# Output weights and affine residual rows: where in the kernel they are prepared

## The chip, the cores and the metric

One core of a Trainium2 chip runs the whole program in one launch. Its engines are TensorE (PE: matmuls; PEld: its weight loads), VectorE (DVE), ScalarE (ACT), GpSimd (POOL) and SyncE (SP); in this kernel SP and POOL mostly issue DMA transfers. The metric is the device time of one execution in microseconds (us). The kernel before took 2729.65 us, the median of three runs (2724.99 to 2732.59).

## What is computed

A decoder trunk of two layers over 1024 rows of width 1024, in float32. Each layer is a token mixer followed by a dense MLP, each in a residual LayerNorm:

```python
for i in range(DEPTH):
    shift, scale, gate = ada_mod(c, ada_w[i, 0], ada_b[i, 0])
    h = x * (1.0 + scale) + shift
    y = mixer_a(h, ...) if i % N_MIXERS == 0 else mixer_b(h, b_w_qkv[j], b_w_out[j], slopes)
    x = layer_norm(ALPHA * x + gate * y, ln_g[i, 0], ln_b[i, 0])
    shift, scale, gate = ada_mod(c, ada_w[i, 1], ada_b[i, 1])
    h = x * (1.0 + scale) + shift
    y = squared_relu_mlp(h, mlp_w_up[i], mlp_w_down[i])
    x = layer_norm(ALPHA * x + gate * y, ln_g[i, 1], ln_b[i, 1])
```

The change lies in the second layer's mixer, an attention with three window patterns:

```python
def mixer_b(h, w_qkv, w_out, slopes):
    qkv = (h @ w_qkv).reshape(B, S, N_PAT, 3, B_HEADS, B_HEAD_DIM)
    for g, (window, dilation) in enumerate(B_PATTERNS):
        o, lse = dilated_branch(qkv[:, :, g, 0], qkv[:, :, g, 1], qkv[:, :, g, 2], window, dilation, slopes)
    wts = jax.nn.softmax(jnp.stack(lses, axis=0), axis=0)[..., None]
    o = jnp.sum(wts * jnp.stack(outs, axis=0), axis=0)
    return o.reshape(B, S, B_HEADS * B_HEAD_DIM).astype(h.dtype) @ w_out
```

Two things of it matter here. `w_out` (called `b_w_out` in the kernel) is multiplied by the gate before the product, since `gate * (o @ w_out)` is `o @ (w_out * gate)`. And the residual `ALPHA * x` is rebuilt from rows that were stored normalised but without LayerNorm's gain and bias: `row * (ALPHA * ln_g[0, 1]) + ALPHA * ln_b[0, 1]`. These last are the affine rows.

## The kernel before

**Numbers in two parts.** Each float32 operand of a matmul is split into a high part (a ScalarE cast, line 102) and a low part (a VectorE subtraction, line 103); a product is three matmuls, high by high, high by low and low by high. `split` is that helper, so many groups in the profile have lines 102 and 103, and the tile's name tells them apart.

**The stages.** First the mixer of layer one, then its MLP (`psua`, `psd` in the profile), then `values`, then `attention`, then `go_on` and the second MLP.

**`values`** makes v for three patterns, and q and k of the first, from the rows of h as products of 2 by 2 blocks with seven instead of eight block products. `V_STEPS` lists 35 steps: five groups (three of v, one of q, one of k) of seven products in the order 1, 2, 5, 6, 7, 4, 3. A step has four blocks `m` of 12 matmuls each into `psv`. While a step runs, the right-hand blocks of the next are subtracted and split (`prepare`) and those of the one after are loaded by SP (`load`, into `raw_tile` buffers). `evict` empties PSUM: after products 1, 5 and 6 by a ScalarE copy alone, after 2, 7, 4 and 3 into a tile of `parted` (two buffers), split, and stored to DRAM by POOL (`v_dram`, `qk_dram`). The generator `second` builds the left-hand forms S1 to S4 and L22 in 17 steps. The four tiles `l21` are held to the end of the stage, where they become the form L21 that attention needs.

**`attention`** runs by a calendar written out by hand. There are 24 groups `n` (eight pairs of heads by three patterns), eight slots each, and ten slots at the end; each slot has two halves. `at(slot, half)` and `in_half(half_slot)` enter functions; within a half they run by rank. `project` makes q and k of the other two patterns and is stepped by a credit in every half slot. For each group there are `load_v`, the scores, `soften` (bias, minimum, exponential), `transposes`, `halve` (`pThi` on ScalarE, `pTlo` on VectorE), `weighted` (the `pv` matmuls) and `gather` into a tile `oT`, of which there are four buffers.

When the three groups of a pair are done, `merge` joins them: `read` loads the statistics, `factors` computes weights and stores them (`w_dram`), `spread` loads them as rows (`bc`, three buffers of the tag "res"), and twelve steps `scale`, `add` and `cut` follow from half slot 18 after the merge's base, at every second half slot, for the last two pairs at every one. `in_order` pins an instruction behind the one traced before it on its engine. For the last pair those twelve steps are not in the calendar; `go_on` runs them.

**Affine rows** (lines 1661 to 1686): eight tiles of 128 rows are loaded from `spill[1]` early in attention, scaled and shifted by VectorE in slots 1 to 23, and stored back by POOL. `accumulate` later adds them to the residual by an accumulating DMA.

**Output weights** (lines 1696 to 1729): eight units, one for each pair of heads. `staged_unit` loads a raw tile, multiplies it by the row `gate_2` (in an `oT` buffer) and splits it, at slots counted from `last_group` (184). Units 6 and 7 are split in `go_on`.

**The output product** is `accumulate`: `psoa` (rows of half 0, pairs 0 to 3) and `psob` (half 1, pairs 0 and 1) are stepped in the calendar from slot 176 on; `psoc` (half 1, pairs 2 and 3) and `psod` (half 0, pairs 4, 5, 6 and then 7) run in `go_on`; `psoe` beside the second MLP's start.

Of the kernel before, what the change touches and what calls it, by code (L numbers as in the profile page):

```python
# [10 lines left out]
F32 = mybir.dt.float32  # L11
# [6 lines left out]
P = 128  # L18
# [17 lines left out]
def trunk(ctx: ExitStack, tc: tile.TileContext, x, c, ada_w, ada_b, ln_g, ln_b, a_w_in, a_b_in,  # L36
# [1037 lines left out]
    qk_dram = dram.tile([N_PAIRS, 2, P, 2, S], F32, name="qk_0")  # L1074

# [55 lines left out]
    def values(before, right, ahead):  # L1131
# [3 lines left out]
        with ExitStack() as ph:  # L1135
# [15 lines left out]
            l21 = [hold.tile([P, HALF], F32, name=f"l21_{k}") for k in range(4)]  # L1151
# [21 lines left out]
            def second():  # L1173
# [7 lines left out]
                for k in range(4):  # L1181
                    h_row(k, l21[k][:])
# [3 lines left out]
                    V.tensor_tensor(s1[:], l21[k][:], x22[k][:], op=ALU.add)  # L1186
# [5 lines left out]
                for k in range(4):  # L1192
                    s3 = x_tile(f"s3_{k}")
                    sub(s3[:], form["L11"][:, 0, k, :], l21[k][:])
# [6 lines left out]
                    yield  # L1201
                built.add("S2")
# [33 lines left out]

            for n, (g, X, p) in enumerate(V_STEPS):
# [34 lines left out]
    def attention(form):  # L1272
# [5 lines left out]
        with ExitStack() as ph:  # L1278
# [104 lines left out]
            def attend(n, oT_of):  # L1383
# [6 lines left out]
                @at(base + 1, 0)  # L1390
# [178 lines left out]
            def merge(hp, oTs):  # L1569
# [15 lines left out]
                @at(*((base + 4, 0) if hp < N_PAIRS - 1 else (base + 1, 0)))  # L1585
                def factors():
# [3 lines left out]
                    in_order(V.tensor_tensor(m[:], nm[:, 0], nm[:, 1], op=ALU.min))  # L1590
# [15 lines left out]
                @at(*((base + 4, 1) if hp < N_PAIRS - 1 else (base + 1, 0)))  # L1606
# [54 lines left out]
            affine = {}  # L1661

            def affine_load(i):
                if i == 0:
                    for n, src in (("g", ln_g), ("b", ln_b)):
                        affine[n] = row_bc(f"aff_{n}")
                        nc.sync.dma_start(affine[n][:], src[0, 1].partition_broadcast(P))
                t = affine[i] = vec.tile([P, S], F32, name=f"aff_{i}", tag="oT", bufs=4) if i < 4 else row_bc(f"aff_{i}")
                nc.sync.dma_start(t[:], spill[1][i * P : (i + 1) * P, :])

            def affine_scale():
                for n in "gb":
                    A.mul(affine[n][:], affine[n][:], ALPHA)

            def affine_row(i):
                t = affine[i]
# [181 lines left out]
```

## Time and profile before

| | us |
|---|---|
| median of three runs | 2729.65 |
| the profiled execution | 2727.96 |
| its span, first to last instruction | 2726.2 |
| TensorE busy in the span | 2658.8 |
| VectorE busy | 1989.8 |
| ScalarE busy | 1377.1 |

How rows are read: a group has line, engine, operation, names (written <- read), shape and count, then busy time in us, mean ns of one, and the idle time of the engine just before them with what ended it. A row of a stretch has its length, the busy time of each engine with the number of instructions, the granted TensorE clock (1.00 is full), the busy share of the DMA engines and GB/s. A row of the timeline begins with start and duration. A row of waits has the sum, the number and the longest.

### The profile page before, as it was taken

The numbers are of one execution on the slowest core, as the hardware profiler recorded it, in microseconds if no ns is written. First come the engines' busy times: TensorE is split into PE (matmuls) and PEld (weight loads), VectorE is DVE, ScalarE is ACT, GpSimd is POOL, SyncE is SP. The second block draws the span as 40 slices with busy tenths as digits, with TensorE's granted clock in tenths as the row PEclk, the third lists the DMA queues.
The fourth block names the chain that finished last, engine by engine and source line by source line (L and its number), as shares of the span: only waits on it lengthen the run. The fifth ranks groups of instructions, "written<-read, shape, count | busy, mean of one in ns | idle before, by whom it ended". The sixth has DMA issues, their size and how long they took to land.

```text
span 2726.2 us, 36911 instructions
## 1 busy us (share of the span) xinstructions
PE 2658.8 (98%) x13242; PEld 2196.3 (81%) x13242; DVE 1989.8 (73%) x3594; ACT 1377.1 (51%) x2593; POOL 97.0 (4%) x161
## 2 busy tenths in 40 slices
PE   6999999999999999999999999999999999999998
PEld 5788888887888878888888888888777788878886
DVE  6787698787867778555557767777768966577877
ACT  3354375555443464434436666666655655554332
POOL 1000000000000000111110000000010000000000
PEclk9999999999999999999999999999999999999999
DMA  7534346667936545655565554555672654485562
GB/s 263 159 118 134 116 140 224 227 214 257 333 131 194 195 155 193 212 186 182 178 210 153 155 140 129 132 144 139 193 183 105 202 189 159 149 311 192 171 207 86
DMA packets 332572, 487.98 MB, mean 179 GB/s; under 512 B 50988, under 2 KB 176340, under 8 KB 332388
## 3 DMA queue, kind: packets, MB, share of 16 engines
q1 hardware_dynamic: 318564, 435.29, 50.3%
q0 software_dynamic: 13824, 50.34, 5.2%
q8 instruction: 104, 1.70, 0.3%
q14 instruction: 80, 0.66, 0.1%
HBM read 357.01 MB, written 128.53 MB: 178 GB/s over the span
## 4 chain that ended last, share of the span: by engine, by line
PE 77%; DVE 12%; DMA 6%; ACT 3%; issue 2%; SPq 1%; DVEq 0%; ACTq 0%
PE psd L955 22%; PE psv L1257 13%; PE psua L796 7%; PE psq L1358 6%; PE psk L1358 6%; DMA adaw<-in_ada_w_dram 3%; PE psuc L796 3%; PE psd_wout L389 3%; PE psu L368 3%; PE pv L1527 3%; PE sc L1447 2%; PE psv L470 2%; PE psub L796 2%; DVE adaacc L128 1%; DVE left L103 1%
## 5 line engine op out<-in xcount | busy, mean ns | idle before, releaser
L796 PE MATMUL psua<-right,left 128*128 128x512 f32 x1536 | 363.4, 390 | 0.3
L955 PE MATMUL psd<-rhi,lhi 128*128 128x512 f32 x896 | 349.9, 390 | 3.0 <-ACT part L827 3.0
L955 PE MATMUL psd<-rlo,lhi 128*128 128x512 f32 x896 | 349.6, 390 | 0.2
L955 PE MATMUL psd<-rhi,llo 128*128 128x512 f32 x896 | 349.2, 390 | 0.0
L796 PEld LDWEIGHTS psua<-right,left 128*128 128x128 f32 x1536 | 287.1, 188 | 61.7 <-DVE right L103 1.4
L1469 ACT ACTIVATE p<-p,stat 128x128 f32<-128x128 f32 (+1 forms) x384 | 168.7, 441 | 107.8 <-DVE stat L1467 104.7
L955 PEld LDWEIGHTS psd<-rhi,lhi 128*128 128x128 f32 x896 | 168.6, 188 | 39.1 <-ACT part L827 3.9
L955 PEld LDWEIGHTS psd<-rlo,lhi 128*128 128x128 f32 x896 | 168.5, 188 | 35.9 <-DVE rlo L103 1.1
L955 PEld LDWEIGHTS psd<-rhi,llo 128*128 128x128 f32 x896 | 168.6, 188 | 35.0
L796 PE MATMUL psuc<-right,left 128*128 128x512 f32 x768 | 187.2, 390 | 0.0
L128 DVE SCALAR_TENSOR_TENSOR adaacc<-adaw,silu_c,adaacc 128x512 f32<-128x512 f32 x168 | 128.5, 775 | 55.0 <-DMA adaw<-in_ada_w_dram 54.6
L796 PEld LDWEIGHTS psuc<-right,left 128*128 128x128 f32 x768 | 143.5, 188 | 30.0 <-DVE right L103 0.4
L103 DVE TENSOR_TENSOR pTlo<-pT,pThi 128x512 fp32r<-128x512 f32 (+1 forms) x160 | 99.3, 621 | 75.1 <-ACT pThi L102 74.1
L103 DVE TENSOR_TENSOR left<-ws,left 128x512 fp32r<-128x512 f32 x128 | 87.8, 688 | 71.5 <-ACT left L102 69.7
L103 DVE TENSOR_TENSOR llo<-lraw,lhi 128x1024 fp32r<-128x1024 f32 x112 | 136.4, 1218 | 0.8 <-ACT lhi L102 0.8
L102 ACT CAST left<-ws 128x512 fp32r<-128x512 f32 x128 | 79.1, 620 | 99.1 <-DVE ws L717 87.8
L1358 PE MATMUL psk<-form_L,wqk_hi 128*128 128x512 f32 x384 | 127.0, 412 | 0.0
L1358 PE MATMUL psq<-form_L,wqk_hi 128*128 128x512 f32 x384 | 126.4, 410 | 0.0
L102 ACT CAST rhi<-rraw 128x1024 fp32r<-128x1024 f32 x48 | 50.6, 1053 | 139.6 <-issue 113.7
L1257 PE MATMUL psv<-vrhi,form_S 128*128 128x512 f32 x384 | 119.9, 390 | 0.6 <-ACT vrhi L102 0.4
L102 ACT CAST lhi<-lraw 128x1024 fp32r<-128x1024 f32 x112 | 117.4, 1048 | 3.5 <-PE psua L796 3.5
L1467 DVE CUSTOM_DVE_ANT_0 p<-sc,bias 128x128 f32<-128x128 f32 (+1 forms) x384 | 113.6, 346 | 6.7 <-PE sc L1447 5.8
(326 smaller groups left out, 6094.4 us busy)
## 6 DMA issues: line engine op xcount, KB each, us to landing
lraw<-forms SPq DMA_DIRECT2D x112, 512.0 KB
adaw<-in_ada_w_dram SPq DMA_DIRECT2D x192, 256.0 KB
up<-in_mlp_w_up_dram SPq DMA_DIRECT2D x64, 512.0 KB
forms<-s SPq DMA_DIRECT2D x128, 256.0 KB
rraw<-in_mlp_w_down_dram SPq DMA_DIRECT2D x64, 512.0 KB
forms<-part SPq DMA_DIRECT2D x96, 256.0 KB
v<-vs POOLq DMA_DIRECT2D x48, 512.0 KB, 3.7
vraw<-in_b_w_qkv_dram SPq DMA_DIRECT2D x42, 512.0 KB
```

The source lines that it names most:

```text
L102: first = A.copy(hi, src) if hi_engine is A else hi_engine.tensor_copy(hi, src)
L103: return first, lo_engine.tensor_tensor(lo, src, hi, op=ALU.subtract)
L128: ins = V.scalar_tensor_tensor(acc[:], raw[:], silu_c[:, k : k + 1], acc[:], ALU.mult, ALU.add)
L368: T.matmul(dst, s[a], m[b], start=(n == 0), stop=(n == last))
L389: T.matmul(p[:], stat[a][:, k, o : o + P], u[b][:, w], start=n == 0, stop=n == count - 1)
L796: T.matmul(acc, w[:, a, k, :], right[p][:, b, k, :], start=p in (1, 2, 5) and k + a + b == 0, stop=k == 3 and a == 1, skip_group_check=True)
L955: ins = T.matmul(sums[kind, m][:], l[a][:, k, m * P : (m + 1) * P], r[b][:, k, :], start=p in (1, 5, 2, 3) and kp + k + a + b == 0, stop=k ...
L1257: T.matmul(acc, rows[:, m * P : (m + 1) * P], cols_, start=p in (1, 2, 5) and kp + k + a + b == 0, stop=kp == 1 and k == 1 and a == 1, ski ...
L1358: T.matmul(p[:], wu[a][:, k * P : (k + 1) * P], h_op(k, half, b), start=k + c_ == 0, stop=k == KD - 1 and c_ == 2)
L1467: V.tensor_tensor_reduce(out=pr, in0=banks[e][:, sl], in1=st["bias"][:, width - w :], scale=-0.125, scalar=3e38, op0=ALU.add, op1=ALU.min, ...
L1469: A.activation(pr, pr, AF.Exp, bias=nm, scale=-1.0, accum_out=l)
L1527: T.matmul(pvs[b][:, q0 % HALF : q0 % HALF + w_], stt, x_[:, o_ : o_ + w_], start=not begun[b], stop=left[b] == 0, skip_group_check=True)
```

## The change

In `values`, the four `l21` tiles become two tiles of the tag "side" (two buffers of the same size together). Once S3 is built they are stored to DRAM (`x21_dram`), and in the last group they are loaded back for the form L21. In between the two buffers serve 24 pieces: from step 5 on, at the first block of each step except steps 28 to 31, the piece begun in the step before is finished and the next is begun. A weight piece is 128 rows by 512 columns of `b_w_out`: load, product with the gate row, split, one store of both parts. A row piece is 256 rows by 512 columns of the affine rows: load, product and sum for each 128 rows, store back. The first vector instruction of each is pinned.

In `attention`, the affine functions and `staged_unit` are gone. `load_unit` loads finished parts into tiles: units 0, 1, 2 and 4 into buffers of the weight tags, 3 into the two "raw" buffers, 7 into a buffer of the tag "v", 5 and 6 late, where units 0 and 1 lay. `load_v` moves from slot 1 of its group to one slot before it, the merge steps from half slot 18 to 22, and the last merge's `factors` and `spread` by half a slot, with the first of the factors pinned.

```diff
+    wo_dram = dram.tile([N_PAIRS, P, 2, 2, HALF], F32, name="wo_parts")
+    x21_dram = dram.tile([2, P, 2, HALF], F32, name="x21")
...
-            l21 = [hold.tile([P, HALF], F32, name=f"l21_{k}") for k in range(4)]
+            side = [hold.tile([P, 2, HALF], F32, name=f"l21_{k}", tag="side", bufs=2) for k in range(2)]
+            l21 = [side[k // 2][:, k % 2, :] for k in range(4)]
...
+                for k in range(2):
+                    nc.gpsimd.dma_start(x21_dram[k], side[k][:])
                 built.add("S2")
...
+            def row_halves(*srcs):
+                across.clear()
+                for src in srcs:
+                    across.append(work.tile([P, HALF], F32, name=f"row_{len(across)}", tag="h"))
+                    nc.sync.dma_start(across[-1][:], src.partition_broadcast(P))
...
+            def weight_piece(k, dh):
+                if k + dh == 0:
+                    row_halves(gate_dram[2, 0:HALF], gate_dram[2, HALF:])
+                t = side_tile(f"wo_{k}_{dh}")
+                nc.sync.dma_start(t[:, 1], b_w_out[0, k * P : (k + 1) * P, dh * HALF : (dh + 1) * HALF])
+                yield
+                in_order(V.tensor_tensor(t[:, 1], t[:, 1], across[dh][:], op=ALU.mult))
+                split(t[:, 0].bitcast(F32R), t[:, 1].bitcast(F32R), t[:, 1])
+                nc.gpsimd.dma_start(wo_dram[k, :, dh, :, :], t[:])
+
+            def row_piece(i, dh):
+                w = slice(dh * HALF, (dh + 1) * HALF)
+                if i == 0:
+                    row_halves(ln_g[0, 1, w], ln_b[0, 1, w])
+                t = side_tile(f"aff_{i}_{dh}")
+                src = spill[1][2 * i * P : 2 * (i + 1) * P, w].rearrange("(n p) c -> p n c", p=P)
+                nc.sync.dma_start(t[:], src)
+                yield
+                if i == 0:
+                    for r in across:
+                        in_order(A.mul(r[:], r[:], ALPHA))
+                for n in range(2):
+                    in_order(V.tensor_tensor(t[:, n], t[:, n], across[0][:], op=ALU.mult))
+                    V.tensor_tensor(t[:, n], t[:, n], across[1][:], op=ALU.add)
+                nc.gpsimd.dma_start(src, t[:])
+
+            pieces = deque([weight_piece(k, dh) for k in range(N_PAIRS) for dh in range(2)] + [row_piece(i, dh) for dh in range(2) for i in range(4)])
...
+                if n == 5:
+                    run(stream)
...
+                    if n > 4 and m == 0:
+                        for _ in range(len(begun)):
+                            next(begun.popleft(), None)
+                        if pieces and n not in (28, 29, 30, 31):
+                            begun.append(pieces.popleft())
+                            next(begun[-1])
...
-                        place("L21", m, l21[m][:])
+                        place("L21", m, back[m // 2][:, m % 2, :])
+                    if (g, X) == V_STEPS[-1][:2] and p == 2 and m < 2:
+                        back.append(side_tile(f"back_{m}"))
+                        nc.sync.dma_start(back[m][:], x21_dram[m])
...
-                @at(base + 1, 0)
+                @at(max(0, base - 1), 0)
                 def load_v():
...
-                @at(*((base + 4, 0) if hp < N_PAIRS - 1 else (base + 1, 0)))
+                @at(*((base + 4, 0) if hp < N_PAIRS - 1 else (base + 1, 1)))
                 def factors():
...
-                    in_order(V.tensor_tensor(m[:], nm[:, 0], nm[:, 1], op=ALU.min))
+                    tc.keep_in_program_order(V.tensor_tensor(m[:], nm[:, 0], nm[:, 1], op=ALU.min))
...
-                @at(*((base + 4, 1) if hp < N_PAIRS - 1 else (base + 1, 0)))
+                @at(*((base + 4, 1) if hp < N_PAIRS - 1 else (base + 1, 1)))
                 def spread():
...
-                    n = pace * n + 18
+                    n = pace * n + 22
...
-            staged_unit(0, (-14, 0), (-12, 0), (-11, 0))
...
-            late = [staged_unit(6, (9, 0), (11, 1), None), staged_unit(7, (9, 1), (12, 1), None)]
+            def load_unit(k):
+                if k == 7:
+                    t = qp.tile([P, 2, D], F32R, name="wo_7", tag="v")
+                    ending["units"][k] = tuple(t[:, i, :] for i in range(2))
+                else:
+                    ending["units"][k] = tuple(wts.tile([P, D], F32R, name=f"wo_{k}_{m}", tag="raw" if k == 3 else f"w{m}", bufs=2 if k == 3 else 4)[:] for m in ("hi", "lo"))
+                for i, t in enumerate(ending["units"][k]):
+                    nc.sync.dma_start(t.rearrange("p (d c) -> p d c", c=HALF).bitcast(F32), wo_dram[k, :, :, i, :])
+
+            for k, half_slot in ((3, -34), (0, -32), (1, -30), (2, -27), (4, -15), (7, 11), (5, 17), (6, 18)):
+                in_half(2 * last_group + half_slot, 4)(lambda k=k: load_unit(k))
...
-                for f in late:
-                    f()
```

More of the change, by code (lines that the diff above doesn't have):

```diff
@@ L1181, in second @@
                 for k in range(4):
-                    h_row(k, l21[k][:])
+                    h_row(k, l21[k])
                     x22.append(x_tile(f"l22_{k}"))
@@ L1193, in second @@
                     s3 = x_tile(f"s3_{k}")
-                    sub(s3[:], form["L11"][:, 0, k, :], l21[k][:])
+                    sub(s3[:], form["L11"][:, 0, k, :], l21[k])
                     plus_lo("L11", k, s3[:])
@@ L1658, in attention @@
                 merge(hp, oTs)
[L1661 to L1676, printed above, removed]
-                for n, op in (("g", ALU.mult), ("b", ALU.add)):
-                    tc.keep_in_program_order(V.tensor_tensor(t[:], t[:], affine[n][:], op=op))
-                nc.gpsimd.dma_start(spill[1][i * P : (i + 1) * P, :], t[:])
-            at(0, 0)(affine_scale)
-            for i in range(NT):
-                if i > 3:
-                    at(5 * i - 15, 0)(lambda i=i: affine_load(i))
-                at(*((i + 1, 1) if i < 4 else (5 * i - 12, 1)))(lambda i=i: affine_row(i))
             last_group = 8 * (len(order) - 1)
```

37 lines of the change are left out of this document (6 added, 31 removed).

## Prediction

> **What bounds the kernel now.** I read the page first, then busy time by stage, then TensorE's waits in the stages that were not full, and last the timelines around each wait.
>
> ```profile
> span 2726.2 us, 36911 instructions
> ...
> PE 2658.8 (98%) x13242; PEld 2196.3 (81%) x13242; DVE 1989.8 (73%) x3594; ACT 1377.1 (51%) x2593; POOL 97.0 (4%) x161
> ...
> PE 77%; DVE 12%; DMA 6%; ACT 3%; issue 2%; SPq 1%; DVEq 0%; ACTq 0%
> ```
>
> TensorE is busy 98% of the span and holds 77% of the chain. No matmul is added or removed, so only TensorE's idle time and its slow clock can change, in either direction.
>
> ```profile
> core 0: us, PE busy (x) PEld busy (x) DVE busy (x) ACT busy (x) POOL busy (x), PEclk, DMA share, GB/s
> 991.00:1377.00 386.00, 385.36 (x1714) 318.24 (x1713) 248.09 (x311) 171.65 (x244) 47.83 (x80) 1.00 0.57 197
> ...
> 1900.00:1982.00 82.00, 75.10 (x495) 62.65 (x496) 60.56 (x178) 48.32 (x143) 2.21 (x6) 0.96 0.65 199
> 1982.00:2033.00 51.00, 48.55 (x291) 40.19 (x290) 29.57 (x83) 34.26 (x87) 7.70 (x10) 0.97 0.77 162
> ```
>
> These are busy times by stage. The block products of v run from 991 to 1377 us and leave TensorE 0.64 us idle: nothing can be won where the work is put, only lost. The end of attention is idle for 6.9 us and 2.45 us, with a granted clock under 1. Finer stretches place this:
>
> ```profile
> 1519.00:1521.00 2.00, 1.23 (x11) 0.96 (x10) 2.00 (x7) 0.61 (x3) 0.00 (x0) 1.00 0.40 116
> 1594.00:1596.00 2.00, 0.84 (x7) 0.58 (x6) 2.00 (x6) 0.14 (x1) 0.00 (x0) 1.00 0.07 17
> 1957.00:1979.00 22.00, 15.10 (x107) 12.14 (x106) 18.33 (x40) 11.93 (x31) 0.00 (x0) 0.92 0.85 266
> 2027.00:2033.00 6.00, 3.79 (x21) 2.92 (x20) 5.86 (x12) 3.92 (x6) 0.35 (x1) 0.81 0.80 181
> ...
> 1969.30:1972.70 3.40, 3.06 (x13) 2.46 (x12) 3.40 (x4) 3.14 (x8) 0.00 (x0) 0.50 0.24 70
> 1979.50:1982.90 3.40, 3.40 (x11) 2.74 (x11) 3.40 (x15) 1.41 (x4) 0.00 (x0) 0.50 1.10 391
> 2030.70:2037.50 6.80, 6.23 (x18) 4.94 (x18) 5.45 (x10) 0.84 (x2) 0.00 (x0) 0.50 0.60 173
> ```
>
> Window length less PE busy: 0.77, 1.16, 6.90 and 2.21 us idle, 11.0 us in all. The last three rows are stretches at half clock, each right behind a group of waits: 13.6 us at 0.50 do 6.8 us of work and so cost another 6.8 us. The prize is at most 11.0 + 6.8 = 17.8 us.
>
> **The change, part by part.** First who holds TensorE there.
>
> ```profile
> PE pv L1527 <- ACT pThi L102: 3.3, 1, 3.3
> PE pv L1527 <- DVE pTlo L103: 3.1, 3, 2.3
> ...
> 1516.02 1.09 DVE L1623 TENSOR_TENSOR bc<-oT,bc 128x512 f32<-128x512 f32 x1 [3.52 <-DMA bc<-w_dram]
> ...
> 1963.92 1.98 DVE L1623 TENSOR_TENSOR bc<-oT,bc 128x512 f32<-128x512 f32 x2 [1.97 <-DMA bc<-w_dram]
> ...
> 1965.99 1.07 ACT L1536 COPY oT<-pv 64x512 f32<-64x512 f32 x2 [2.69 <-DVE bc L1623]
> ...
> 1969.09 1.21 DVE L1712 TENSOR_TENSOR wo_raw<-wo_raw,gate 128x1024 f32<-128x1024 f32 x1
> 1970.22 1.21 DVE L103 TENSOR_TENSOR wo_lo<-wo_raw,wo_hi 128x1024 fp32r<-128x1024 f32 x1
> ...
> 1976.36 1.21 DVE L1712 TENSOR_TENSOR wo_raw<-wo_raw,gate 128x1024 f32<-128x1024 f32 x1
> ```
>
> The wait rows are of 1957 to 1979 us. VectorE takes its instructions in order. At 1516 and again at 1963.9 it stands at merge's pinned `scale` until the broadcast `bc` lands; behind it stand the `pTlo` halves that the pv matmuls need. At 1965.99 ScalarE's copy into `oT` waits for that same scale: five claims share the four `oT` buffers, since `gate_2` holds one. From 1969 to 1978 two gate products and two `wo_lo` stand in front of `pTlo`.
>
> *Merge two slots later* (18 to 22 half slots).
>
> ```profile
> 1415.29 1.48 PE sc L1447 x24
> ...
> 2032.97 13.16 PE psoc L1756 x48
> ```
>
> The first scores and the end of the slots, in the chain: (2032.97 - 1415.29) / 194 = 3.2 us a slot, so 6.4 us of delay against stalls of 3.52 and 1.97 us. The early waits go: 0.77 + 1.16 = 1.9 us. Bounds 0 and 1.9; I take 1.9. The merge's result is read again slots later and covers the delay, except in the last merge (below).
>
> *Weights and affine rows out of attention.* Removed there, from the groups by line:
>
> ```profile
> L1678 DVE TENSOR_TENSOR aff<-aff,aff_g 128x1024 f32<-128x1024 f32 x8 | 9.8, 1219 | 0.0
> L1712 DVE TENSOR_TENSOR wo_raw<-wo_raw,gate 128x1024 f32<-128x1024 f32 x8 | 9.7, 1218 | 0.7 <-DMA wo_raw<-in_b_w_out_dram 0.6
> L103 DVE TENSOR_TENSOR wo_lo<-wo_raw,wo_hi 128x1024 fp32r<-128x1024 f32 x8 | 9.6, 1215 | 0.5 <-ACT wo_hi L102 0.4
> ```
>
> With the additions, like the products 9.8 us, that is 38.9 us of VectorE work in attention. Its worth is not 38.9 us but what stood in front of `pTlo`. At 1957 to 1979 us the gate tile, the four instructions and the early scale all go: of 6.9 us idle I keep 0.5 and take 6.4 (bounds 0 and 6.9), and with it the two half-clock stretches, 3.4 us. Moved merge steps now meet the first `psoa` products instead, and some waiting returns: 0 to 5.6 us (both long waits again, 3.3 + 2.3), I take 2.
>
> *The last two slots.* Two `wo_lo` and the factors of the last merge stood among the last `pTlo`; the weights go and the factors are pinned behind. Idle 2.2 us, I take 1.7, and the half clock behind it, 3.4 us. But the last merge then follows later or equal:
>
> ```profile
> 2025.36 0.17 DVE L1590 TENSOR_TENSOR mm<-mst 128x16 f32<-128x16 f32 x1
> ...
> 2028.59 1.23 DVE L103 TENSOR_TENSOR wo_lo<-wo_raw,wo_hi 128x1024 fp32r<-128x1024 f32 x1
> ...
> 2041.39 1.09 DVE L1623 TENSOR_TENSOR bc<-oT,bc 128x512 f32<-128x512 f32 x1
> ...
> 2048.64 2.35 DVE L103 TENSOR_TENSOR wo_lo<-wo_raw,wo_hi 128x1024 fp32r<-128x1024 f32 x2
> ...
> 2054.05 1.47 DVE L103 TENSOR_TENSOR oTs<-bc,oTs 128x512 fp32r<-128x512 f32 x2
> ```
>
> Unit 7 needs `oTs` of the last pair after psoc (48 matmuls) and 36 of psod: at 0.227 us (13.16 us hold 2.2 us of half clock, so 10.9 / 48) that is 19.1 us after psoc begins; before, 2032.97 + 13.16 + 8.2 = 2054.3, just met. After, psoc begins near 2032.97 - 1.7 - 1.1 (half clock from 2030.7 on) = 2030.2, so the need is at 2049.3. The factors start behind the last `pTlo`, about 4 us later, but nothing then stands between them: by the two 1.2 us `wo_lo` and the `pTlo` they let pass, their result is there 0.4 us earlier. Less the 2.35 us of `wo_lo` after the scale, `oTs` is near 2054.05 - 0.4 - 2.35 = 2051.3. Bounds 0 (psoc's evictions, now earlier, are out of the scale's way) and 5.4 us (first half of `oTs` at 2054.7 as before); I take 2.
>
> *The pieces beside the products.* 16 weight pieces (product, subtraction, one ScalarE cast) and 8 row pieces (four VectorE passes), all 128x512:
>
> ```profile
> L102 ACT CAST vs<-vpart 128x512 fp32r<-128x512 f32 x36 | 22.4, 621 | 55.7 <-DVE vpart L1223 28.5 <-DMA v<-vs 19.0 <-DVE vraw L1110 4.6
> ...
> L103 DVE TENSOR_TENSOR vs<-vpart,vs 128x512 fp32r<-128x512 f32 x36 | 24.8, 688 | 11.0 <-ACT vs L102 11.0
> ...
> 1202.70:1213.60 10.90, 10.90 (x49) 9.02 (x49) 5.68 (x7) 3.02 (x5) 1.59 (x3) 1.00 0.73 242
> 1235.40:1246.30 10.90, 10.90 (x50) 9.03 (x49) 10.01 (x12) 3.99 (x6) 1.41 (x2) 1.00 0.12 50
> ...
> its engine sat idle before it (us, times) until:
>   DMA v<-vs: 43.8, 21
> ...
> DMA to landing us min/median/max: 2.8/3.7/6.2
> ```
>
> (16 x 2 + 8 x 4) x 0.688 = 44 us more VectorE, 248 to 292 of 386 us (76%); 10 us more ScalarE. The worst step holds 10.01 of 10.9 us; a row piece puts it at 12.8, and the lighter steps beside it (5.68) take the 1.9 us up. The pinned product holds back evictions behind it only if its load is late, and that load was issued a step (10.9 us) earlier against a slowest landing of 6.2. SP issues 24 loads, 6 row broadcasts and the 2 returns of x21 between the loads of v; POOL 26 stores between those of v. Bytes: 16 x 0.75 + 8 x 1 + 2 (x21) + 1.5 (rows) = 23.5 MiB, 64 GB/s more on 197. Cost 0 to 25 us (rival C); since TensorE waited only 0.64 us here under stores as late as 6.2 us, I take 1.
>
> *At nothing:* v loaded two slots earlier (its tile is free, its use 7 slots later); 16 finished 512 KB unit loads, for 8 raw ones, five slots or more ahead of use, except units 5 and 6 after psob's last reader, with all of psoc (10.9 us) for 2 MB, some 8 us at the 266 GB/s above. Uncovered they would cost up to 8 us at psod. The stream run out at the sixth V step is empty by then: its 17 steps are taken in the first four.
>
> **Sum:** -1.9 - 6.4 - 3.4 + 2 - 1.7 - 3.4 + 2 + 1 = **-11.8 us**. The profiled execution took 2727.96 us (span 2726.2 and 1.8 around it), so 2716.2; it lies 1.7 us under the median of 2729.65, which moves to **2718 us**.
>
> **The rivals.**
> A, *everything goes*: no new wait, all 17.8 us gone: 2712. For it: VectorE has room in every later stretch. Against: the merge chain had no slack.
> B, *the wait moves to unit 7*: the chain of the last merge stays as late as 2054.7, the wait is 5.4 instead of 2 us and the clock halves once more for 6.8 us (3.4 us): -11.8 + 3.4 + 3.4 = -5, 2725. The w_dram and bc transfers behind 2 MB of units speak for it.
> B2, *the half clock has another cause* and stays: -11.8 + 6.8 = -5, 2725. Against it: each stretch follows waits. The Trainium skill, TensorE: Matmul & The Clock Gate (Why this matters for your kernels), asks for no idle gap over about 3 us; only the 3.3 us wait is that long, so by the rule one stretch (1.7 us of cost) would go and the sum be -6.7, 2723. The trace has half clock right behind a 2.3 us wait, against the rule.
> C, *stores of v back up*: two `vs` buffers take twelve stores in a row in steps 7, 4 and 3. A buffer's round is landing + cast + subtraction, 3.7 + 0.62 + 0.69 and an estimated 0.5 between them = 5.5 us for two blocks of 2.72 us: balanced today. At a landing of 6.2 it is 8.0, 48 us for a 32.7 us train; less the step of 10.9 us by which evictions may lag before a PSUM bank is written again, TensorE loses 5 us in each of five trains, 25 us: 2743. It decides from a landing of about 5.3 us. For it: a step at 242 GB/s and 0.73 share gets a weight piece's 0.75 MiB, 72 GB/s more, share 0.95. Against: weight pieces store once in a step, and the share reached 1.10 at 391 GB/s. The Trainium skill, DMA: Bandwidth & Descriptors (Issuing engines are not separate DMA queues), says that transfers from all issuers share the same 16 engines, so POOL's stores get no lane of their own; no row here contradicts it.
>
> **How the numbers follow.** Chances: forecast 0.46, A 0.14, B 0.13, B2 0.12, C 0.15. The forecast's own range is 2713 to 2723. The range 2709 to 2735 leaves out most of C and the edge of A. I count 0.3% (8.2 us, to 2721.5) as what can be told from no change: faster 0.60 (A and most of the forecast), same 0.28 (B, B2, its edge), slower 0.12 (most of C).
>
> **What would show it.** Right: no DVE wait on `bc`, no `wo_raw` or `aff` after 1377, granted clock 1.00 from 1900 to 2033, v stage still 386 us. Unit 7's wait would be on psod from `oTs`. Wrong: psv waiting for `vrhi`, landings of v over 5 us, or psoa waiting for a unit's load.

## The result, and the profile after

The changed kernel takes **2718.03 us** (median of seven runs, 2714.43 to 2723.03) against 2729.1 us for the kernel before (seven runs): a ratio of **0.9958, 95% interval 0.9944 to 0.9972**, 11.1 us less where 2718 and 11.8 us less were forecast. Two later sets of runs of the same order of instructions gave 0.9963 and 0.9972 (e1_again, e11_units_late), so the gain is 6 to 11 us by the medians. Two executions of the experiments, one of e2 and the profiled one of e3, took 1.6 and 2 times as long as the rest and are left out, so e3 has no stage times.

The profiled execution of the changed kernel is the slowest of its seven, 2723.03 us; that of before took 2727.96. The two spans differ by 4.9 us only, so the traces are compared by stage.

From the page after:

```profile
PE 2658.1 (98%) x13242; PEld 2195.5 (81%) x13242; DVE 1993.1 (73%) x3626; ACT 1378.6 (51%) x2603; POOL 104.7 (4%) x179
```

The same matmuls, busy for the same time; what changed is when TensorE waits. Stage borders come from the rows of single tiles (durations, then the start of the first and of the last): the first `psv` of `values`, the first `psq` of attention, the last merge's load of `mst`, the first `psoe`. Before, then after:

```profile
L1257 PE MATMUL psv<-vrhi,form_L x288: 389/389/478, 991.2 to 1213.6; 128*128 128x512 f32 x144
...
L1358 PE MATMUL psq<-form_L,wqk_hi x384: 387/393/506, 1377.0 to 1939.2; 128*128 128x512 f32 x192
...
L1582 SPq DMA_DIRECT2D mst<-st_dram x24: 359/372/2031, 1431.5 to 2022.1; - x24
...
L1756 PE MATMUL psoe<-wo_hi,oTs x64: 388/389/478, 2067.8 to 2095.4; 128*128 128x512 f32 x64
```

```profile
L1306 PE MATMUL psv<-vrhi,form_L x288: 388/389/478, 994.3 to 1217.6; 128*128 128x512 f32 x144
...
L1416 PE MATMUL psq<-form_L,wqk_hi x384: 387/393/506, 1385.7 to 1943.6; 128*128 128x512 f32 x192
...
L1640 SPq DMA_DIRECT2D mst<-st_dram x24: 359/366/552, 1440.2 to 2018.6; - x24
...
L1761 PE MATMUL psoe<-wo_hi,oTs x48: 389/393/497, 2064.3 to 2090.0; 128*128 128x512 f32 x48
```

| stretch | before | after | difference | forecast |
|---|---|---|---|---|
| start to first `psv` (untouched) | 991.2 | 994.3 | +3.1 | 0 |
| `values`: first `psv` to first `psq` | 385.8 | 391.4 | +5.6 | +1 |
| attention: first `psq` to the last `mst` | 645.1 | 632.9 | -12.2 | -9.7 |
| last merge: `mst` to first `psoe` | 45.7 | 45.7 | 0.0 | -3.1 |
| `psoe` to the end | 658.4 | 657.0 | -1.4 | 0 |
| span | 2726.2 | 2721.3 | -4.9 | -11.8 |

(-9.7 is -1.9 - 6.4 - 3.4 + 2; -3.1 is -1.7 - 3.4 + 2.) The first row is no work of the change: over the thirteen profiles that can be read this untouched stretch took 988.0 to 995.2 us.

One border misleads. The load of `mst` is issued by SyncE, and it moved against TensorE's work: it stands 10.6 us ahead of the first `psoc` before and 5.6 us after. The rows of `psoc`, and busy times from the first `psq` to the first `psoc`, before and then after (length, then PE, PEld, DVE, ACT, POOL, the granted clock, DMA share, GB/s):

```profile
L1756 PE MATMUL psoc<-wo_hi,oTs x32: 389/389/735, 2032.8 to 2045.7; 128*128 128x512 f32 x32
...
1377.00:2032.80 655.80, 643.27 (x4202) 538.43 (x4201) 453.39 (x1338) 400.39 (x1165) 34.78 (x67) 0.99 0.57 155
```

```profile
L1761 PE MATMUL psoc<-wo_hi,oTs x32: 389/389/443, 2024.2 to 2034.9; 128*128 128x512 f32 x32
...
1385.70:2024.20 638.50, 636.79 (x4202) 535.04 (x4200) 420.38 (x1301) 394.52 (x1157) 27.19 (x59) 1.00 0.56 153
```

By TensorE's own borders, first `psq` to first `psoc` took 655.7 us and now takes 638.5, 17.2 less, and TensorE is idle there for 1.7 instead of 12.5 us. First `psoc` to first `psoe` took 35.1 and now takes 40.1, 5.1 more. The forecast, split there, is -12.5 (-1.9 - 6.4 - 3.4 + 2 - 1.7 - 1.1) and -0.3 (the other 2.3 us of half clock, and + 2). So more was won ahead of `psoc`, and more lost behind it, than the table shows: its 0.0 hides a loss of 5 us.

Busy times by stage, after:

```profile
991.00:1377.00 386.00, 382.01 (x1690) 314.80 (x1689) 287.06 (x376) 181.14 (x263) 61.76 (x104) 1.00 0.71 249
...
1900.00:1982.00 82.00, 82.00 (x559) 69.31 (x559) 55.87 (x180) 49.12 (x153) 3.25 (x8) 1.00 0.74 225
```

From 1900 to 1982 us TensorE went from 75.10 of 82 us at clock 0.96 to 82.00 of 82 at 1.00: the hole is gone. Two new holes stand in its place.

**The first new hole is in `values`.** Windows around it, and the timeline of all engines, both of the changed kernel:

```profile
1300.00:1312.00 12.00, 12.00 (x55) 9.94 (x54) 8.33 (x12) 1.91 (x4) 2.06 (x4) 1.00 0.96 326
...
1320.50:1323.90 3.40, 3.40 (x8) 2.72 (x9) 3.37 (x4) 0.71 (x2) 0.72 (x1) 0.50 1.00 380
```

```profile
1311.30 0.62 ACT L102 CAST qs<-vpart 128x512 fp32r<-128x512 f32 x1 [5.70 <-DMA qk<-qs]
...
1311.95 0.69 DVE L103 TENSOR_TENSOR qs<-vpart,qs 128x512 fp32r<-128x512 f32 x1 [3.63 <-ACT qs L102]
1312.56 0.69 DVE L1279 TENSOR_TENSOR aff<-aff,row 128x512 f32<-128x512 f32 x1
...
1318.02 0.68 DVE L1279 TENSOR_TENSOR aff<-aff,row 128x512 f32<-128x512 f32 x1
1318.62 0.68 DVE L1278 TENSOR_TENSOR aff<-aff,row 128x512 f32<-128x512 f32 x1
1319.22 1.22 DVE L103 TENSOR_TENSOR vrlo<-vraw,vrhi 128x1024 fp32r<-128x1024 f32 x1
...
1320.50 0.80 PE L1306 MATMUL psv<-form_L,vrlo 128*128 128x512 f32 x1 [2.80 <-DVE vrlo L103]
```

From the top, all engines in order of time: a store of `qs` lands late at a DMA share of 0.96; ScalarE's cast, which needs the buffer back, waits 5.70 us; VectorE, in order, stands 3.63 us behind the cast, and then two row pieces' passes stand among the work it has to catch up, ahead of the `vrlo` that TensorE needs. After the 2.80 us wait the clock is 0.50 for 3.40 us, another 1.7 us.

**The second is unit 7's wait.** Timelines of SP, DVE and PE of the changed kernel, at the end of attention:

```profile
2018.60 0.36 SPq L1640 DMA_DIRECT2D mst<-st_dram  x1
2019.06 0.55 SPq L1731 DMA_DIRECT2D wo_lo<-wo_parts  x1
2019.70 1.22 SPq L1731 DMA_DIRECT2D wo_hi<-wo_parts  x2
2020.97 1.00 SPq L1731 DMA_DIRECT2D wo_lo<-wo_parts  x1
2026.63 1.49 SPq L1662 DMA_DIRECT2D w_dram<-ma  x3
2032.47 3.69 SPq L1669 DMA_DIRECT2D bc<-w_dram  x6
```

```profile
2037.74 1.08 DVE L1681 TENSOR_TENSOR bc<-oT,bc 128x512 f32<-128x512 f32 x1 [5.77 <-DMA bc<-w_dram]
...
2041.52 3.28 DVE L1681 TENSOR_TENSOR bc<-oT,bc 128x512 f32<-128x512 f32 x4
2044.70 2.50 DVE L1685 TENSOR_TENSOR bc<-bc,bc 128x512 f32<-128x512 f32 x4
```

```profile
2047.31 4.88 PE L1761 MATMUL psod<-wo,oTs 128*128 128x512 f32 x12 [3.42 <-ACT oTs L102]
```

The factors' store is issued at 2026.63 and the first load of `bc` only 5.84 us later (before: 2032.12 to 2036.49, 4.37 us). Then VectorE takes the scales of both halves before it adds anything, though unit 7's first rows need one half only: the kernel writes all six steps of one half ahead of those of the other, but pins them for the other pairs and not for the last. That is no new order: before, too, five of the six scales ran ahead of the first addition (2041.39 to 2050.92). TensorE waits 3.42 us, and half clock follows (twelve matmuls in 4.88 us; in e6_pin below, without it, 3.31).

### The profile page after: what moved, and what is told of

Its sections match the earlier page's. It is cut to its first block, busy times and chain, and to the rows that moved or that the text cites. A ratio compares the mean times of both kernels' runs of the same rounds, so it can differ in the third digit from the quotient of the medians.

```text
span 2721.3 us, 37097 instructions
## 1 busy us (share of the span) xinstructions
PE 2658.1 (98%) x13242; PEld 2195.5 (81%) x13242; DVE 1993.1 (73%) x3626; ACT 1378.6 (51%) x2603; POOL 104.7 (4%) x179
## 4 chain that ended last, share of the span: by engine, by line
PE 45%; DVE 4%; issue 2%; DMA 2%; ACT 1%; POOL 0%; SPq 0%; DVEq 0%; POOLq 0%; ACTq 0%
PE psd L955 11%; PE psk L1416 7%; PE psq L1416 7%; PE psua L796 5%; PE pv L1585 3%; PE sc L1505 3%; PE psv L1306 2%; PE psuc L796 2%; PE pT L1558 1%; PE psub L796 1%; PE psoa L1761 1%; PE psoe L1761 1%; PE pT L1561 1%; PE psod L1761 0%; DVE right L103 0%
```

## The experiments

Medians of before in the four sets of runs beside the experiments: 2728.07, 2727.75, 2727.88 and 2729.43 us. The stretches of each profile, between the same borders (worked out from times to a hundredth, so a last digit may differ from the table above):

| kernel | median us | ratio to before | `values` | attention to `mst` | `mst` to `psoe` |
|---|---|---|---|---|---|
| before | | | 385.9 | 645.1 | 45.7 |
| changed | 2718.03 | 0.9958 [0.9944, 0.9972] | 391.4 | 632.9 | 45.7 |
| e1_again | 2718.96 | 0.9963 [0.9948, 0.9978] | 391.2 | 634.8 | 46.3 |
| e2_merge18 | 2720.13 | 0.9964 [0.9951, 0.9976] | 387.5 | 635.4 | 46.1 |
| e3_before_merge22 | 2727.41 | 0.9992 [0.9979, 1.0005] | - | - | - |
| e4_no_rows | 2712.88 | 0.9934 [0.9913, 0.9955] | 386.6 | 633.1 | 45.4 |
| e5_rows_dma | 2721.99 | 0.9978 [0.9966, 0.9989] | 395.0 | 634.2 | 45.9 |
| e6_pin | 2713.95 | 0.9950 [0.9932, 0.9967] | 390.8 | 633.0 | 41.4 |
| e7_skip27 | 2713.88 | 0.9947 [0.9930, 0.9965] | 386.8 | 634.2 | 45.6 |
| e8_pin_skip | 2713.04 | 0.9945 [0.9926, 0.9965] | 387.3 | 634.7 | 44.1 |
| e9_passes_back | 2718.74 | 0.9960 [0.9946, 0.9975] | 388.3 | 636.4 | 43.1 |
| e10_claim | 2716.04 | 0.9951 [0.9936, 0.9966] | 388.3 | 632.7 | 45.2 |
| e11_units_late | 2721.90 | 0.9972 [0.9959, 0.9984] | 391.1 | 632.5 | 45.6 |
| e12_all_back | 2726.41 | 0.9993 [0.9982, 1.0005] | 390.5 | 642.0 | 44.2 |

### e1_again: are the two new holes there each time?

> The changed kernel once more, for a second profile. If the two give-backs belong to the kernel, they stand again in the same places: a wait of 2 to 3 us for vrlo in the last group of the block products (stage 390 to 392 us from the first to the last psv, against 386 before) and one of 3 to 4 us for oTs in psod. If they were chance, the stage is 386 to 387 us and psod has no wait. Median 2714 to 2721 us, ratio to before 0.994 to 0.998.

The changed kernel once more. The same two waits stood at the same places: 2.24 us for `vrlo` with half clock behind it, 2.96 us on `psod`. `values` took 391.2 us against 385.9 before. That they stand there is the change's, not chance. How long they are varies: over the eight profiles with `values` as in the changed kernel (this one, the first, e2, e6 and e9 to e12) the longest wait for `vrlo` is 0.87 to 2.94 us and the stage 387.5 to 391.4.

### e2_merge18 and e3_before_merge22: what the later merge is worth

```diff
-                    n = pace * n + 22
+                    n = pace * n + 18
```

> The changed kernel with the merge steps back at half slot 18. Theory 1 (the weights and the gate tile leaving attention carry the gain, the later merge only the early waits): VectorE waits for bc again near the ninth slot of the first merges, 2 to 4 us slower than the changed kernel, ratio to before 0.996 to 0.998. Theory 2 (the later merge carries the gain): 8 us or more slower than the changed kernel, ratio 0.999 or above.

> The kernel before with only the merge steps moved from half slot 18 to 22. Theory 1: the two early waits (1.9 us) go, but the copy into oT of the last pair waits for the scale of the merge before, since the gate row holds one of the four buffers, and that scale is now 6 us later: TensorE idles longer near 1965 us, 2 to 8 us slower than before, ratio 1.001 to 1.003. Theory 2: the stalls on bc go and with them most of the idle time, 6 to 11 us faster than before, ratio 0.996 to 0.998.

In the changed kernel with the merge back at 18, two early waits return (0.77 us at 1522.6 and 0.54 at 1610.6), and attention up to `mst` takes 635.4 us against 632.9 and 634.8: 0.6 to 2.5 us. In the kernel before, the merge at 22 alone gives 0.9992 with an interval across 1. So the shift carries little of the gain by itself; that it would cost 2 to 8 us in the kernel before, where five claims share four `oT` buffers, was wrong as well.

### e4_no_rows: what the row pieces cost `values`

```diff
-... + [row_piece(i, dh) for dh in range(2) for i in range(4)])
+...)
```

It leaves out the gain and bias of the affine rows.

> The changed kernel without the eight row pieces (the residual rows of the second layer go without gain and bias, 22 us of VectorE and 8.4 MB of transfers each way left out). Theory 1 (VectorE and the stores of the row pieces hold up vrlo in the last group): the wait for vrlo goes, the block products take 386 to 388 us, 3 to 5 us faster than the changed kernel. Rival (the weight pieces cost as much): the stage stays at 390 us or above.

2712.88 us. (The eight pieces move 4.2 MB each way, 8.4 MB in all, not 8.4 each way as expected above.) TensorE's longest group of waits in `values` in this kernel:

```profile
PE psv L1306 <- DVE vpart L1228: 0.6, 2, 0.4
```

The wait for `vrlo` is gone, and 386.6 us are 0.7 more than before: the sixteen weight pieces cost little. The eight row pieces cost the rest, 4.8 us in the profiled pair (391.4 - 386.6), 3.3 against the mean of the eight profiles (389.9).

### e5_rows_dma: vector passes or traffic?

```diff
-                if i == 0:
-                    for r in across:
-                        in_order(A.mul(r[:], r[:], ALPHA))
-                for n in range(2):
-                    in_order(V.tensor_tensor(t[:, n], t[:, n], across[0][:], op=ALU.mult))
-                    V.tensor_tensor(t[:, n], t[:, n], across[1][:], op=ALU.add)
```

The row pieces are loaded and stored with nothing done to them.

> The changed kernel with the row pieces loaded and stored as they are but without their VectorE passes and the two ScalarE scalings (the residual rows go without gain and bias). If VectorE's eight passes in front of vrlo are the cause of the wait at the second step of the last group, the wait goes, as in the kernel without row pieces (block products 387 us, median 2712 to 2715 us). If the traffic of the row pieces (late landings of the qk stores) is the cause, a wait of 1.5 us or more and 389 us or more stay. If it takes both, the wait goes and the longest qk landing stays near 7 us.

It was slower, 2721.99 us, `values` 395.0: neither theory, and no clean split. Timelines of POOL, ACT and DVE, POOL's waits and the timeline of PE in this kernel say why:

```profile
1250.69 0.72 POOL L1274 DMA_DIRECT2D spill<-aff  x1 [9.26 <-DMA aff<-spill]
...
1253.97 0.71 POOL L1234 DMA_DIRECT2D qk<-qs  x1
...
1259.80 0.62 ACT L102 CAST qs<-vpart 128x512 fp32r<-128x512 f32 x1 [11.50 <-DMA qk<-qs]
...
1260.45 0.69 DVE L103 TENSOR_TENSOR qs<-vpart,qs 128x512 fp32r<-128x512 f32 x1 [10.64 <-ACT qs L102]
```

```profile
POOL spill L1274 <- DMA aff<-spill: 46.0, 8, 10.6
```

```profile
1261.80 0.79 PE L1300 MATMUL psv<-form_S,vrhi 128*128 128x512 f32 x1 [6.89 <-DVE vpart L1228]
```

Without its passes a row's store comes earlier in POOL's queue and waits there for its own load, up to 10.6 us. Here two of them wait 9.26 and 1.82 us, and a store of q, whose data VectorE had finished by 1243.69, is issued behind them at 1253.97. ScalarE waits 11.50 us for its `qs` buffer, VectorE 10.64 for ScalarE, TensorE 6.89 for VectorE. Here the chain of rival C ran to the end: late store, cast, VectorE, TensorE. What the passes and what the traffic alone cost stays open.

### e6_pin: the order of the last merge

```diff
                 def in_order(ins):
-                    if hp < N_PAIRS - 1:
-                        tc.keep_in_program_order(ins)
+                    tc.keep_in_program_order(ins)
```

> The changed kernel with the twelve steps of the last merge pinned in the order in which they are written, half 0 before half 1. Theory (VectorE takes all six scales before the first cut, so unit 7's oTs come a half too late): the wait for oTs in psod falls from 3 to under 1 us, the half clock behind it goes, psod takes 22.5 to 24.5 us instead of 28, 3 to 5 us faster than the changed kernel. Rival (the landing of bc sets it): the wait stays at 2 to 3 us.

2713.95 us. Timelines of DVE and PE:

```profile
2037.56 0.69 DVE L1680 TENSOR_TENSOR bc<-oT,bc 128x512 f32<-128x512 f32 x1 [1.08 <-DMA bc<-w_dram]
2038.29 1.42 DVE L1684 TENSOR_TENSOR bc<-bc,bc 128x512 f32<-128x512 f32 x2
...
2040.39 0.69 DVE L103 TENSOR_TENSOR oTs<-bc,oTs 128x512 fp32r<-128x512 f32 x1
2041.00 2.65 DVE L1680 TENSOR_TENSOR bc<-oT,bc 128x512 f32<-128x512 f32 x3
```

```profile
2040.41 3.31 PE L1760 MATMUL psod<-wo,oTs 128*128 128x512 f32 x12 [1.10 <-ACT oTs L102]
```

The first half is added and cut before the second is scaled; the wait falls from 3.42 to 1.10 us, no half clock follows, and `mst` to `psoe` falls from 45.7 to 41.4 us. The order is not all of it: in e8 below, with the same order, the wait is 2.50 us.

### e7_skip27 and e8_pin_skip: row pieces away from the end of q

```diff
-                        if pieces and n not in (28, 29, 30, 31):
+                        if pieces and n not in (27, 28, 29, 30, 31):
```

> The changed kernel with step 27 left free of a piece, so that the last two row pieces come in steps 32 to 34. Theory (two row pieces meet the stores of steps 25 to 28): the wait for vrlo falls under 1 us, block products 386 to 388 us, 3 to 5 us faster than the changed kernel. Rival (any row piece in the train of stores does it): the wait stays over 1.5 us, or moves to the last steps.

> Both: the last merge pinned and step 27 left free. If the two give-backs are separate, the gains add up: 6 to 10 us faster than the changed kernel, 2709 to 2713 us, ratio to before 0.993 to 0.994.

With no piece begun in step 27, one row piece fewer stands in the crowded stretch around 1310 us: `values` takes 386.8 us and 387.3, without the long wait, though stores of q landed as late as 8.5 us in e7, and VectorE stood as long behind the cast as in the changed kernel (3.63 us there):

```profile
1305.77 0.69 DVE L103 TENSOR_TENSOR qs<-vpart,qs 128x512 fp32r<-128x512 f32 x1 [3.71 <-ACT qs L102]
```

So the late store alone does no harm; it takes the second row piece behind it. The kernel with both edits took 2713.04 us. It was expected at the sum of both gains, and gives no more than either. Its profiled execution, at 2720.01 us the slowest of its four, still waits 2.50 us on `psod`, though the steps run in the pinned order. There VectorE waits for `bc` ahead of each of the three scales of the first half, as in e6 but longer (5.7 us together instead of 4.3); the third:

```profile
2041.32 0.69 DVE L1680 TENSOR_TENSOR bc<-oT,bc 128x512 f32<-128x512 f32 x1 [1.39 <-DMA bc<-w_dram]
```

In this execution it was the landing of `bc`, the rival of e6, that set the wait. The ratio of e8 lies below that of the changed kernel, but the intervals overlap; only the stretches separate them.

### e9_passes_back, e10_claim and e12_all_back: what the hole in attention was made of

Twelve vector passes on finished units at the old slots (e9); the gate row in a fifth claim on `oT` (e10); both with the old merge and the ScalarE casts (e12). The core of e9:

```diff
+            def stand_in(slot, half, k):
+                @at(last_group + slot, half)
+                def again():
+                    hi = ending["units"][k][0]
+                    t = hi.bitcast(F32)
+                    tc.keep_in_program_order(V.tensor_tensor(hi, t, t, op=ALU.max))
```

The core of e10, with a small store that reads the tile at the end:

```diff
+            @at(last_group - 13, 0)
+            def claim():
+                held["gate"] = vec.tile([P, D], F32, name="gate_2", tag="oT", bufs=4)
+                nc.sync.dma_start(held["gate"][:], gate_dram[2].partition_broadcast(P))
```

> The changed kernel with VectorE's weight passes put back into attention and nothing else: twelve pinned 128x1024 passes (the larger of a number and itself, so that the unit stays as it is) on finished units, at the slots where the kernel before had its gate products and low parts of units 0 to 5. The gate tile, the early merge and the affine rows stay out. Theory 1 (these passes in front of the low parts of the weights of attention were the wait at 1957 to 1979 us): TensorE waits for pTlo again between about 1940 and 1975 us, 3 to 6.5 us, with half clock behind it, and the kernel takes 2721 to 2729 us. Theory 2 (the wait was the fifth claim on four oT buffers or the early merge, and the passes were only seen beside it): TensorE stays full there, 2716 to 2720 us.

> The changed kernel with the gate row loaded into one of the four oT buffers again, claimed at the old slot and held until the merge of the last pair, with no vector work on it. Theory 1 (passes): the copy into oT waits for the merge's scale, but TensorE hardly does; 2716 to 2721 us. Theory 2 (five claims on four buffers, and the merge now two slots later): the pv banks stay occupied until the scale of the pair before, TensorE waits 3 to 10 us in slots 176 to 182 (about 1955 to 1985 us), 2722 to 2735 us.

> The changed kernel with all that attention lost of the output weights put back together: the twelve vector passes of before (with the ScalarE casts of the high parts ahead of six of them), the gate row in a fifth claim on the oT buffers, and the merge at half slot 18. Each alone gave back little: from the first q product to the first of psoc 643.4 us with the passes, 638.9 with the claim, 640.9 with the early merge, 638.5 with none and 655.7 before. Theory 1 (the long waits need them together: the early scale stands and waits, the copy into oT waits for it through the fifth claim, and the passes follow it): waits of 2 to 3.5 us at pThi and pTlo between 1945 and 1980 us, half clock behind them, 648 to 657 us for that stretch, 2723 to 2730 us in all. Theory 2 (they only add up, and the rest was held by something else that the change moved, the affine rows, the loads of v or the factors' place): 644 to 647 us for that stretch, 2717 to 2722 us in all.

The same window in the three kernels, e9, e10 and e12:

```profile
1900.00:1982.00 82.00, 80.24 (x529) 66.44 (x528) 61.80 (x175) 47.84 (x148) 5.15 (x10) 1.00 0.78 236
```

```profile
1900.00:1982.00 82.00, 82.00 (x546) 69.13 (x545) 55.34 (x174) 50.06 (x153) 5.38 (x10) 1.00 0.85 251
```

```profile
1900.00:1982.00 82.00, 78.44 (x513) 64.96 (x512) 60.63 (x172) 49.52 (x146) 3.17 (x7) 0.98 0.77 239
```

And TensorE's waits from 1900 to 2033 us in e12:

```profile
PE psoa L1788 <- DVE wo_hi L1755: 3.1, 2, 2.5
PE pv L1586 <- DVE pTlo L103: 2.9, 4, 1.3
```

The passes alone bring back 1.76 us of idle time in this window, less than the 3 to 6.5 expected of them, and the claim alone none; so each of these two runs spoke against its own suspect as the single cause. All together bring back 3.56 us there with a clock under 1, and the whole kernel goes back to 2726.41 us, a ratio of 0.9993. From the first `psq` to the first `psoc`, the stretch of the expectation, e12 takes 650.1 us, in the range of theory 1: 11.7 us of the 17.2 that the change had won there. (Up to `mst` it is 9.1 of 12.2.) Alone the parts give 4.9 (passes), 0.4 (claim) and 2.4 us (merge), 7.7 in sum; the eight profiles with attention as in the changed kernel vary by 2.2 us (638.5 to 640.7). So the parts seem to need each other, but e12 also has six ScalarE casts that none of the single runs has, and what these alone do was not tried. In its mechanism theory 1 was wrong: no copy into `oT` waited for the scale in e12, and the 3.3 us wait that ran through it before did not return. VectorE's own queue made e12's waits, and the longest, 2.5 us, is `psoa` waiting for one of the passes put back. The wait of before through the fifth claim is not reproduced, and 5.5 us of the gain ahead of `psoc` stay without a shown cause; the affine rows, the loads of v and the place of the factors, which the change moved as well, were not put back.

In e9 the time does not rise, although attention is 3.5 us longer: `mst` to `psoe` is 2.6 us shorter there, with a wait of 1.41 us on `psod` in place of 3.42. Time lost ahead of the last merge is time in which the transfers ahead of its store drain: the store takes 3.9 us there instead of 5.84 (see e11).

### e11_units_late: the factors' store behind the units' loads

```diff
-            ..., (7, 11), (5, 17), (6, 18)):
+            ..., (7, 11), (5, 19), (6, 19)):
```

> The changed kernel with the loads of units 5 and 6 moved behind the last merge's loads of bc in SP's order. Theory 1 (the store of the factors and the loads of bc stand behind 2 MB of unit loads): from the store's issue to the first load of bc 4 to 4.6 us instead of 5.8, the scale from w_dram's bc and so oTs 1 to 2 us earlier, the wait on psod 1 to 2 us shorter, 2714 to 2718 us; psod must not wait for units 5 and 6. Theory 2 (the round trip is latency of its own): the same 5.8 us and 3 us of wait, 2717 to 2720; if the units then land late, TensorE waits at psod's first product instead, 2719 to 2723.

The loads are not pinned, and SP issued them where it did without the edit, from 0.46 us after `mst` on. So the run tells nothing of the theories; it is a third run of the changed kernel, 2721.90 us. The question is answered by all twelve profiles read here that load the units in this way (e3 is left out). The first load of `bc` was issued 11.0 to 11.7 us after the last of the units' four loads in every one of them, while the factors' store between them was issued anywhere from 5.35 us (e7) to 7.93 us (e12) after it. The sooner the store followed the units, the longer it took: 6.29 us in e7, 3.43 in e12. The store stands behind 2 MB of unit loads; that is shown by this pattern, not by an edit. The DMA engines agree: in the changed kernel they are full for 4 us from the store's issue on, and nearly idle (share 0.09) in the last 1.9 us before the first load of `bc`:

```profile
2026.60:2030.60 4.00, 4.00 (x19) 3.34 (x18) 2.79 (x6) 0.00 (x0) 0.00 (x0) 1.00 0.97 295
2030.60:2032.50 1.90, 1.90 (x10) 1.55 (x9) 0.70 (x2) 0.00 (x0) 0.00 (x0) 1.00 0.09 12
```

One limit: the units always follow `mst` by the same half microsecond, so the pattern dates the end of the traffic and does not by itself say whose it is. Before, with two raw loads of 512 KB issued 2.3 us ahead of it, the store took 4.37 us.

## Why the prediction was right, point by point

**The hole in attention** (-1.9 - 6.4 - 3.4 + 2 = -9.7). Right in place and sign, under in size: -12.2 up to `mst`. Up to the first `psoc`, with the 1.7 us and 1.1 of half clock of the last two slots, -17.2 where -12.5 was forecast. The idle time that was kept (0.5 us in the hole, 0.5 in the slots) did not stay, and the 2 us for moved merge steps did not come: VectorE waits once more at a scale in the slots, and no TensorE row waits for it:

```profile
DVE bc L1681 <- DMA bc<-w_dram: 3.1, 1, 3.1
```

The working named the gate tile, the four vector instructions and the early scale together; e12 shows that putting them back (with the casts) undoes most of it, and e9, e10 and e2 that the passes, the claim and the early merge do not do it alone. That the fifth `oT` claim was a cause of its own is not borne out.

**The last two slots and unit 7** (-1.7 - 3.4 + 2 = -3.1). Together 0.0 from `mst` on. The idle time and half clock ahead of `psoc` and in it did go (`psoc` 13.16 to 11.0 us), but the wait on `psod` took it all back: 3.42 us, 1.7 of half clock, and 1.16 us at `psoe`, which had no wait before. From `psoc` on that is +5.1 us, where -0.3 was forecast.

The term +2 was mis-sized, 6.3 us instead of 2. Its step that failed is the time of `oTs`, taken over from before with 0.4 us off. Counted from the first `psoc` (2030.2 in the forecast, 2024.2 measured), the factors' store was forecast at 1.5 us and came at 2.4, and the first load of `bc` was forecast 4.37 us behind it and came 5.84 behind it, at 8.2 instead of 5.9. So `oTs` came 23.5 instead of 21.1 us after the first `psoc`, 2.4 later. TensorE needed it 0.6 us later than forecast and could go on from ScalarE's cast, 0.4 us ahead of VectorE's `oTs`; hence 2 + 2.4 - 0.6 - 0.4 = 3.4 us of wait. The half clock behind it and the wait at `psoe` were put at nothing. The order of the scales is no part of this error, since before had it too and it stands in the 2054.05; it is what could be won (2.3 us of the wait in e6). This is much of rival B, whose 2 MB of units is the mechanism that the trace shows. The Trainium skill, DMA: Bandwidth & Descriptors (Issuing engines are not separate DMA queues), says that transfers share the same 16 engines whoever issues them. The runs agree as far as they go: the same small store took 3.4 to 6.3 us by how much of the units' 2 MB was still ahead of it, but both come from SP, so no run here tests two issuers.

**The stage of v** (+1). Mis-sized: +5.6 in the profiled pair, +4.0 as the mean of the eight profiles with this stage unchanged (387.5 to 391.4, mean 389.9). The sum of VectorE's load was right (287 us busy where 292 were forecast), and VectorE's average was not what decided. The working had a row piece's 1.9 us taken up by lighter steps beside it; it did not put a row piece and a late store into the same step. The price stays in the bounds of 0 to 25, at its low end (the working of the 25 gives 48 - 32.7 - 10.9 = 4.4 us a train, so 22 for five, and 2740 instead of 2743); rival C's landing of 5.3 us was not reached, though single stores were later than its 6.2 (landings of the stores of v in the changed kernel):

```profile
DMA to landing us min/median/max: 2.9/4.4/8.0
```

**At nothing.** Right for `load_v` and for units 0 to 4 and 7: no `psoa` or `psod` row waits for a unit's load. Units 5 and 6 were on time too, but not free, since the factors' store waits behind them.

**The total.** The median of the first set of runs came out at the forecast to a tenth, and in part by chance: the repeats lie 1 and 4 us higher, and in the profiled pair the stretches that the change touches give -8.0 us (-4.9 less the 3.1 of the untouched start), not -11.8. Errors of both signs stand in the sum: 4.7 us more won ahead of `psoc` and 1.4 behind `psoe`, against 4.6 us more lost in `values` and 5.4 between `psoc` and `psoe`. That they nearly cancel is luck. The direction and the range held because the hole in attention, the largest term, was found and costed in the right place.

## What to carry to other kernels

Before work is moved beside a full engine, look not at the mean load of its new neighbours but at the one step in which a late store, the in-order queue behind it and the moved work meet; leaving that one step out (e7) took away a 2.8 us wait. A wait cut out ahead of a chain of transfers comes back behind it, unless the chain is shortened too: here pinning the order of twelve steps (e6) won 4.3 us in its stretch in the profiled pair, a quarter of what the whole change won ahead of `psoc`. Where a hole has several causes in one in-order queue, putting them back one at a time shows little; put them back together.

## What was not expected of the hardware

**Half clock does not follow from a wait's length alone.** Waits for `vrlo` of 0.87, 1.52 and 1.94 us left the clock at 1.00 (e2, e10, e9); waits of 2.23, 2.24 and 2.80 us were followed by half clock (e12, e1, changed); but 2.92 and 2.94 us (e11, e6), at the same place, were not. On `psod` waits of 1.10 and 1.41 us were not followed by it, those of 2.50 to 3.45 us were. The clearest case lies outside the change, in the second MLP: TensorE waits for `part` there in every profile, 1.51 or 1.52 us at the same product, and 3.4 us at a clock of 0.50 begin within 1.2 us in five of the thirteen (the changed kernel, e8, e9, e10, e11) and in none of the other eight:

```profile
PE psd L955 <- ACT part L827: 1.5, 1, 1.5
...
2406.00:2409.40 3.40, 3.40 (x9) 2.65 (x9) 3.40 (x6) 0.33 (x1) 0.00 (x0) 0.50 0.98 329
```

The work there is the same in all of them, so a part of what separates two profiles is of this kind, 1.7 us a time, and its cause stays open. The Trainium skill, TensorE: Matmul & The Clock Gate (Why this matters for your kernels), warns of gaps over about 3 us; in these runs 1.5 us could be enough and 2.9 us could be too little.

**Untouched stages vary by 7 us** from execution to execution (988.0 to 995.2 us for the first `psv`), which is more than most edits here were worth: medians of four to ten runs, and stretches of the trace, decided where single times could not.
